# Moving the split of a stream sum behind the last key products' copy, and the gates' bias to the constants, in a one-core encoder block

## The chip, the cores and the metric

The kernel runs on one core of a Trainium2 chip. A core has five engines that run their own instruction queues in order: TensorE (PE, matrix products; PEld is its loading of the fixed operand), VectorE (DVE), ScalarE (ACT), GpSimd (POOL) and SyncE (SP, which here issues most transfers). They wait for each other and for transfers on semaphores. The metric is the device time of one execution in microseconds (us), lower is better. Matrix products accumulate in PSUM, in banks of 128 x 512 float32 values here; a bank is read out ("evicted") by ScalarE or VectorE before another product starts in it.

## The reference, cut to what matters

One block for a sequence of 1024 frames with 16 learned tokens ahead of them (1040 columns), width 1024, all in float32:

```python
h = concatenate([meta, x])                                   # 1040 x 1024
h = h + token_mixer(rmsnorm(h, norm_mix_g))
h = h + channel_mixer(rmsnorm(h, norm_ffn_g))
return rmsnorm(h, norm_final_g)[:, 16:]

# token_mixer: proj = u @ w_in gives, per head,
#   4 mLSTM heads:     q, k (convolution, silu), v, output gate o, and the scalar gates i, f
#   4 retention heads: q, k (rotary), v, output gate g
i_pre = ml_i + ml_b_i
li = 15 * tanh(i_pre / 15)                                   # -1e30 on padding
lf = log_sigmoid(ml_f + ml_b_f)
# a scan over chunks for each head, head_norm, times sigmoid(o) or silu(g), then @ w_out
# channel_mixer: (silu(causal_dwconv(u @ w_up)) * (u @ w_gate)) @ w_down
```

## The kernel before

**Products in three parts.** Each float32 operand is split into a high part (a cast on ScalarE to a shorter float, `AC.copy`) and a low part (the operand less its high part, on VectorE). A product is then three matmuls into one bank: high x high, low x high, high x low (`mm3`, L912, and `mm3s`, L917; the matmuls stand on L913 to L915 and L923 to L925).

**Seven products for eight.** The normalised stream is held transposed as four quarters, "11", "12", "21", "22" (the first digit is the half of the sequence, the second the half of the 1024 channels). Most projections are made with seven products of sums of quarters in place of eight: `ROWS` (L1003) lists which block of the stream each of the products n = 0 to 6 reads: 11, 12, S2, S1, S3, S4, 22. Each product runs in two column chunks (ch0, ch1). It accumulates in a bank of kind x (tag pa or pb) or y (the other). S1 = 22 - 21, and the quarters "21", "11" and "12" are overwritten with further sums (`usum`, L1838; L1843 and L1841 are its two operations on VectorE). `usplit` (L1845) then makes the high part (L1849, ScalarE) and low part (L1850, VectorE) of a sum, in two halves of 128 x 1056 each.

**The stage of the change** (L1786 to L1890, the first 100 us or so). After the norms, the unit runs the products of head 4, the first retention head, without the seven-product scheme: `v4_group` (L945, values and gates, L967) and `q4_group` (L973, i = 0 queries, i = 1 keys). `q4_group` ends with the copy of the bank into `raws[i]`, L979, and leaves that instruction as `last["raw"]`. The last one, for keys and columns 272 to 528 of the second half, is "the last key products' copy". The sums are written in this order: S1 = 22 - 21, then 21, 11 and 12 in place, with the splits of S2 and S1 written ahead of the last `q4_group`s, and those of S3 and S4 after them. S1 lives in the two tiles tagged A1 and A2. A copy of the "12" sum, `x12`, is made into other tiles by ScalarE behind `last["raw"]` (L1869), and S4 is split from it. `tables_load(4)` (L1146, the transfers L1153 and L1154) fills new tiles of the same tags A1 and A2 with the rotary cosines and sines, so the first transfer waits until nobody reads S1 any more.

**The gates.** `gates()` (L1241) turns the i and f columns of all chunks into the scan's weights: two transposes on TensorE (L1258, L1259) into bank pg, a bias scaled by 1/15 (L1262, VectorE), the tanh (L1263, ScalarE, with that bias), the exponential and the logarithm (L1267, L1272), cumulative sums and maxima (L1283, L1285) and transposes (L1290, L1291) with further steps up to L1329. It is a Python generator and is advanced a piece at a time between other work.

**Rotary.** `rotary(i, r)` (L1222) works on head 4's queries (i = 0) and keys (i = 1): two copies on ScalarE that swap the halves of the partitions (L1228, L1229), then two multiplications by the tables A1 and A2 and an addition on VectorE (L1231 to L1233).

**What sets the order.** Instructions written before `pinned[0] = True` (L1888) are put in order by the framework's scheduler, from dependencies and a model of their durations; `after(a, b)` (L105) adds an edge that only keeps a behind b in order and adds no wait if both are on one engine. From L1888 on a hook (`watch`, L132) chains each instruction of TensorE, VectorE and ScalarE to the one written before it on that engine (`before[engine]`), so that order is the written one. `before` is emptied at L1889, so the first of each engine has no predecessor. What is written when is decided by `slot` (L1752) and `go` (L1770): after each step of a product they advance side tasks (gates, rotary, scans) according to the estimated loads of the engines in `load` and the limits in `RULES`. SyncE's and GpSimd's transfers and the instructions written before the pin stay with the framework's scheduler and may be put among pinned ones.

**Weights.** `quartered` (L555) gives the seven weight blocks of a head; `parts` (L472) casts them (L474, `hi_...`) and makes their low parts (L479, `lo_...`), and L567 to L572 make the sums of weights in place. The raw weights of head 4's output gate are raw_o4a and raw_o4b, those of the next head's queries and keys raw_q0a and raw_q0b; a raw tile is loaded again (L328) once its last reader is done. `evac` (L1017) evicts a product's bank: by ScalarE for n = 0, 6 (L1019) and n = 2, 3 (L1021), by VectorE for the others (L1023).

**Start.** L271 loads the vector constants into `vec` from ScalarE's queue, L273 sets one more column of it, and the first VectorE work after that is the square of L859.

## Time and profile before

| | |
|---|---|
| median of 3 runs | 1531.71 us (1531.26 to 1532.25) |
| profiled execution, its own time | 1529.36 us |
| span from the first to the last instruction | 1527.6 us |
| mean granted clock of TensorE | 0.995 |
| busy: TensorE, VectorE, ScalarE | 97%, 71%, 50% of the span |
| TensorE in 72 to 75 us | 1.04 of 3.00 us busy |
| TensorE in 90 to 94.4 us | 0.00 of 4.40 us busy |
| TensorE in 99 to 103 us | 3.20 of 4.00 us busy |

How to read the rows. In a row of the order of time stand the start (us from the span's start), the duration (us), the engine, the line of the kernel, the operation, the tile written <- the tiles read, the shapes, the count, and in brackets how long the engine was idle before and what it then waited for. A name with q, such as SPq, is the engine's queue issuing a transfer. A row with a count over 1 covers several instructions in sequence. In the table of waits stand who waited, for whom, the total in us, how many times, and the longest. In a row by stretches of time stand the length, then busy us and instruction counts of PE, PEld, DVE, ACT and POOL, the granted clock, the share of the transfer engines, and GB/s. The time of a matmul's row is longer than its share of TensorE, since matmuls overlap: the distance between two starts counts. Tile names: rawq and rawk are head 4's queries and keys, sig its output gate, uS1h and uS1l the high and low parts of S1, po4x and po4y the banks of head 4's output products, s the tiles of S1 or of the copied sum, A the rotary tables, gts, gates and gsm the gates' tiles, qT and kT the rotated queries and keys.

### The profile page before, as it was taken

How to read it: one execution, taken by the hardware profiler on the slowest of the kernel's cores; microseconds unless marked ns; L12 is line 12 of the kernel's file. 1: busy time of each engine (PE TensorE's matmuls, PEld its weight loads, DVE VectorE, ACT ScalarE, POOL GpSimd, SP SyncE). 2: the span in 40 equal slices, each digit the busy share in tenths (PEclk: the TensorE clock that was granted, in tenths of full speed). 3: DMA queues.
4: the chain of work that ended last, by engine and by line, in shares of the span. 5: the costliest groups of instructions: out<-in, count | busy, mean ns of one | idle time of the engine just before them, and what ended most of it. 6: DMA issues, size and time to landing. Idle time of an engine off the chain costs nothing.

```text
span 1527.6 us, 25490 instructions
## 1 busy us (share of the span) xinstructions
PE 1488.0 (97%) x9929; PEld 1349.2 (88%) x9929; DVE 1089.4 (71%) x2087; ACT 756.4 (50%) x1455; POOL 72.2 (5%) x157
## 2 busy tenths in 40 slices
PE   7989999999999999999999999999999999999997
PEld 7978999999999999987888988999999999888887
DVE  6875868678777677746868688767666666778657
ACT  4465655554655445553454465444444444434443
POOL 1000000000000000000000001222220000000000
PEclk9999999999999999999999999999999999999999
DMA  6022256323532455697333237778872224933313
GB/s 232 2 85 58 82 166 194 108 80 118 174 131 91 132 166 178 203 385 271 110 110 135 80 119 229 205 201 206 193 185 77 83 77 155 375 102 113 97 42 111
DMA packets 104586, 223.81 MB, mean 147 GB/s; under 512 B 10520, under 2 KB 33760, under 8 KB 104288
## 3 DMA queue, kind: packets, MB, share of 16 engines
q1 hardware_dynamic: 89824, 191.68, 37.7%
q0 software_dynamic: 8448, 23.07, 7.5%
q10 hardware_dynamic: 6192, 7.41, 1.4%
q8 instruction: 78, 1.28, 0.4%
q14 instruction: 44, 0.36, 0.1%
HBM read 178.05 MB, written 67.15 MB: 161 GB/s over the span
## 4 chain that ended last, share of the span: by engine, by line
PE 88%; DVE 6%; DMA 3%; ACT 2%; issue 1%; SPq 0%; ACTq 0%; DVEq 0%
PE pdx L925 3%; PE pdx L924 3%; PE pdx L923 3%; PE pup_x L924 2%; PE pup_x L925 2%; PE pga_x L923 2%; PE pup_x L923 2%; PE pga_x L924 2%; PE pga_x L925 2%; PE pdy L925 2%; PE pdy L924 2%; PE pdy L923 2%; PE n L1621 2%; PE pwx L925 2%; PE u L1619 2%; PE pwx L923 2%
## 5 line engine op out<-in xcount | busy, mean ns | idle before, releaser
L782 ACT CAST hi_up<-raw_up 128x512 fp32r<-128x512 f32 (+1 forms) x52 | 36.5, 719 | 107.7 <-PE pga_z L924 61.1
L783 DVE TENSOR_TENSOR lo_up<-raw_up,hi_up 128x512 fp32r<-128x512 f32 (+1 forms) x52 | 41.2, 809 | 38.3 <-ACT hi_up L782 37.6
L923 PE MATMUL pup_x<-uh_g,hi_up 128*128 128x256 f32 (+1 forms) x240 | 67.2, 282 | 1.2 <-ACT uh_g L1989 1.2
L783 DVE TENSOR_TENSOR lo_ga<-fraw_ga,hi_ga 128x512 fp32r<-128x512 f32 (+1 forms) x52 | 41.8, 807 | 37.1 <-ACT hi_ga L782 36.9
L924 PE MATMUL pup_x<-ul_g,hi_up 128*128 128x256 f32 (+1 forms) x240 | 67.4, 282 | 0.1
L925 PE MATMUL pup_x<-uh_g,lo_up 128*128 128x256 f32 (+1 forms) x240 | 66.4, 282 | 0.0
L783 DVE TENSOR_TENSOR lo_d<-rd,hi_d 128x1024 fp32r<-128x1024 f32 (+1 forms) x34 | 37.6, 1112 | 32.8 <-ACT hi_d L782 32.7
L782 ACT CAST hi_ga<-fraw_ga 128x512 fp32r<-128x512 f32 (+1 forms) x52 | 36.4, 719 | 45.3 <-PE pup_z L924 23.9
L925 PE MATMUL pdx<-uh_d,lo_d 128*128 128x512 f32 (+1 forms) x156 | 57.9, 375 | 0.0
L924 PE MATMUL pdx<-ul_d,hi_d 128*128 128x512 f32 (+1 forms) x156 | 57.8, 374 | 0.0
L782 ACT CAST hi_d<-rd 128x1024 fp32r<-128x1024 f32 (+1 forms) x34 | 32.3, 959 | 49.2 <-PE pdy L924 32.5
L925 PE MATMUL pdy<-uh_d,lo_d 128*128 128x512 f32 x132 | 51.9, 393 | 0.0
L924 PE MATMUL pdy<-ul_d,hi_d 128*128 128x512 f32 x132 | 51.7, 392 | 0.0
L923 PE MATMUL pdx<-uh_d,hi_d 128*128 128x512 f32 (+1 forms) x156 | 48.5, 372 | 0.0
L923 PE MATMUL pdy<-uh_d,hi_d 128*128 128x512 f32 x132 | 47.9, 389 | 0.0
L923 PE MATMUL pga_x<-uh_g,hi_ga 128*128 128x512 f32 x120 | 47.5, 396 | 0.0
L924 PE MATMUL pga_x<-ul_g,hi_ga 128*128 128x512 f32 x120 | 47.5, 396 | 0.0
L923 PEld LDWEIGHTS pup_x<-uh_g,hi_up 128*128 128x128 f32 x240 | 45.3, 189 | 2.3 <-ACT uh_g L1989 1.4
L925 PE MATMUL pga_x<-uh_g,lo_ga 128*128 128x512 f32 x120 | 47.1, 393 | 0.0
L924 PEld LDWEIGHTS pup_x<-ul_g,hi_up 128*128 128x128 f32 x240 | 45.4, 189 | 1.0 <-DVE ul_g L1990 0.3
L925 PEld LDWEIGHTS pup_x<-uh_g,lo_up 128*128 128x128 f32 x240 | 44.7, 189 | 0.8
L1688 DVE SCALAR_TENSOR_TENSOR mx<-tr,vec,sig 128x386 f32<-128x386 f32 (+2 forms) x42 | 24.0, 571 | 21.2 <-PE tr L1680 16.1
(1687 smaller groups left out, 5730.6 us busy)
## 6 DMA issues: line engine op xcount, KB each, us to landing
raw_up<-w_up_d SPq DMA_DIRECT2D x22, 512.0 KB, 4.2
fraw_ga<-w_gate_d SPq DMA_DIRECT2D x22, 512.0 KB, 4.3
acts<-cv SPq DMA_DIRECT2D x44, 256.0 KB, 4.4
wsd<-w_down_d POOLq DMA_DIRECT2D x44, 256.0 KB, 6.6
rd<-wsd SPq DMA_DIRECT2D x22, 512.0 KB, 3.6
raw_w<-w_out_d SPq DMA_DIRECT2D x20, 512.0 KB, 7.5
wsw<-raw_w SPq DMA_DIRECT2D x32, 256.0 KB, 3.7
raw_m<-w_out_d SPq DMA_DIRECT2D x14, 512.0 KB, 4.1
```

The lines of the kernel that those rows point to most:

```text
L782: AC.copy(hi[:, o:o + n], x)
L783: V.tensor_tensor(lo[:, o:o + n], x, hi[:, o:o + n].bitcast(F32), ALU.subtract)
L923: m.append(PE.matmul(pt, ah, xh_, start=first and k == 0, stop=False, skip_group_check=True))
L924: PE.matmul(pt, ah, xl_, start=False, stop=False, skip_group_check=True)
L925: m.append(PE.matmul(pt, al, xh_, start=False, stop=last and k == n - 1, skip_group_check=True))
L1619: PE.matmul(up[:, :nv], kw[:L], v, start=True, stop=True)
L1621: PE.matmul(pn[:L, :nv], pt[:L, :L], v, start=True, stop=c == 0)
L1688: return V.scalar_tensor_tensor(dst, tr[:, x0 - t0:x1 - t0], vec[:, g:g + 1], sig(b, p)[:, x0 - a0:x1 - a0], ALU.mult, ALU.mult)
```

## The change

Three edits, in the diff in full:

1. The split of S1 is written after the last `q4_group` and not before it. Each cast of S1 is kept behind the last key products' copy on ScalarE; each cast and low part of S3 is kept behind the last of S1's on its engine; the copies of the "12" sum are kept behind S3's casts in place of the key copy.
2. The first ScalarE instruction written after the pin is kept behind S1's last cast.
3. The scaled bias of the gates is computed at the start of the kernel into a column of `vec` that was unused, by the same VectorE operation, and `gates()` reads it from there.

```diff
--- before.py
+++ after.py
@@ -271,6 +271,7 @@
     AC.dma_start(vec[:, :V_N], vecs)
     xload(0)
     V.memset(epsc, EPS)
+    V.tensor_scalar(vec[:R36, V_N + 1:V_N + 2], vec[:R36, V_BI:V_BI + 1], 1.0 / 15.0, None, ALU.mult)
     warm = tmp.tile([P, 5], F32, tag="rcol", name="warm")
     AC.activation(warm[:, 0:1], epsc, AF.Sqrt)
     nc.sync.dma_start(cs, cst)
@@ -1258,8 +1259,7 @@
         PE.transpose(pg[:R36, 0:P], gts[:, 0].rearrange("p a b -> p (a b)"), ident)
         PE.transpose(pg[:R36, P:2 * P], gts[:, 1].rearrange("p a b -> p (a b)"), ident)
         li, x, ax, w, lf = row("li"), row("x"), row("ax"), row("w"), row("lf")
-        bi = small(R36, 1)
-        V.tensor_scalar(bi, vec[:R36, V_BI:V_BI + 1], 1.0 / 15.0, None, ALU.mult)
+        bi = vec[:R36, V_N + 1:V_N + 2]
         AC.activation(li, pg[:R36, 0:P], AF.Tanh, bias=bi, scale=1.0 / 15.0)
         V.tensor_scalar(x, pg[:R36, P:2 * P], vec[:R36, V_BF:V_BF + 1], None, ALU.add)
         V.tensor_scalar(ax, x, -1.0, None, ALU.mult)
@@ -1846,15 +1846,19 @@
         ublock_pair(nm, th, tl)
         for i in range(2):
             h_, l_ = (u[:, 2 * i:2 * i + 2] for u in UB[nm])
-            AC.copy(h_, part(x, i))
-            V.tensor_tensor(l_, part(x, i), h_.bitcast(F32), ALU.subtract)
+            m = last["hi", nm] = AC.copy(h_, part(x, i))
+            n = last["lo", nm] = V.tensor_tensor(l_, part(x, i), h_.bitcast(F32), ALU.subtract)
+            if nm == "S1":
+                after(m, last["raw"])
+            elif nm == "S3":
+                after(m, last["hi", "S1"])
+                after(n, last["lo", "S1"])
 
     usum(0, "22", "21", "S1")
     usum(0, "11", "21", "21")
     usum(1, "S1", "11", "11")
     usplit("S2", "11", "r0", "r1")
     usum(1, "11", "12", "12")
-    usplit("S1", "S1", "uh3", "ul3")
     need(("o", 4, 1), 0)
     for i in range(2):
         q4_group(i, 1, 16, 272, next(ring0))
@@ -1862,11 +1866,12 @@
         v4_group(c, next(ring0))
     for i in range(2):
         q4_group(i, 1, 272, SB, next(ring0))
+    usplit("S1", "S1", "uh3", "ul3")
     usplit("S3", "21", "r2", "r3")
     x12 = [vslot(2 + i, f"s4_{i}").rearrange("p (k j) -> p k j", k=2) for i in range(2)]
     tables_load(4)
     for i in range(2):
-        after(AC.copy(x12[i], part("12", i)), last["raw"])
+        after(AC.copy(x12[i], part("12", i)), last["hi", "S3"])
     s1[:] = x12
     need(("o", 4, 1))
     usplit("S4", "S1", "uh2", "ul2")
@@ -1887,6 +1892,7 @@
     done["tr"] = 0.0
     pinned[0] = True
     before.clear()
+    before["Activation"] = last["hi", "S1"].ins.name
     go(o_steps(4))
     for p, (a, b) in enumerate(PAIRS):
         side += sig_tasks(prev) if p else sig_tasks(4)
```

## The prediction

> **What bounds the kernel now.** I read the page's first part, then the table of waits of TensorE, then the time-ordered rows of each engine around the places that table names.

> ```profile
> PE 1488.0 (97%) x9929; PEld 1349.2 (88%) x9929; DVE 1089.4 (71%) x2087; ACT 756.4 (50%) x1455; POOL 72.2 (5%) x157
> ...
> PE po4y L923 <- ACT sig L1021: 4.6, 1, 4.6
> ...
> PE po4x L923 <- ACT rawk L979: 2.0, 1, 2.0
> ```

> TensorE (PE) is busy for 97% of the span, so only its idle time, 1527.6 - 1488.0 = 39.6 us, can be won. The diff touches one stage, about 57 to 103 us, and these two waits lie in it, 4.6 and 2.0 us, with two short ones whose rows come below. The longer is TensorE's wait before n = 5 of head 4's output products, and its rows show what lies behind it:

> ```profile
> 94.41 0.39 PE L923 MATMUL po4y<-uS4h,hi_o 128*128 128x258 f32 x1 [4.57 <-ACT sig L1021]
> 94.00 0.63 ACT L1021 ACTIVATE sig<-po4y 128x256 f32<-128x256 f32 x2
> 92.44 0.36 ACT L1263 ACTIVATE gates<-pg,gsm 36x128 f32<-36x128 f32 x1
> 91.15 1.28 ACT L1263 ACT_TABLE_LOAD   x1 [2.88 <-DVE gsm L1262]
> 90.94 0.13 DVE L1262 TENSOR_SCALAR gsm<-vec 36x1 f32<-36x1 f32 x1
> 88.20 0.71 DVE L1232 TENSOR_TENSOR kT<-kT,A 128x528 f32<-128x528 f32 x1 [2.21 <-DMA A<-rot_d]
> 81.12 0.39 SPq L1154 DMA_DIRECT2D A<-rot_d  x1
> ```

> Read it downward, backwards in time. The bank's eviction stands behind the tanh in ScalarE's (ACT) queue; the tanh waits for a bias that VectorE (DVE) scales at 90.94; VectorE had stood for the second rotary table, issued at 81.12. That table reuses the tile of the stream's first sum, S1, whose casts and low parts come late:

> ```profile
> 71.18 2.05 ACT L1849 CAST uS3h<-x 128x1056 fp32r<-128x1056 f32 x2 [0.57 <-PE pq L915]
> 73.13 1.13 ACT L474 CAST hi_o<-raw_o4b 128x512 fp32r<-128x512 f32 x2
> 74.17 0.36 ACT L979 COPY rawk<-pq 128x256 f32<-128x256 f32 x1
> 74.43 2.05 ACT L1869 COPY s<-x 128x1056 f32<-128x1056 f32 x2
> 76.39 0.36 ACT L1019 COPY sig<-po4x 128x258 f32<-128x258 f32 x1
> 76.65 2.05 ACT L1849 CAST uS1h<-s 128x1056 fp32r<-128x1056 f32 x2
> 78.86 2.06 ACT L1849 CAST uS4h<-s 128x1056 fp32r<-128x1056 f32 x2
> 78.14 2.42 DVE L1850 TENSOR_TENSOR uS1l<-s,uS1h 128x1056 fp32r<-128x1056 f32 x2
> 72.22 0.28 PE L915 MATMUL pq<-u22h,lo_q 128*128 128x256 f32 x1
> ```

> The last key product ends at 72.22 + 0.28 = 72.50, but S3's casts and two weight casts hold its copy until 74.17; that is the 2.0 us wait.

> **The change part by part.** *The key copy.* S3's casts now follow S1's, which follow the copy. The copy can start at 72.50, or, if the two weight casts (73.13 to 74.17, 1.04 us) still go ahead of it, at 73.54. TensorE resumes 0.4 us after a copy starts (74.17 to 74.58), at 72.9 to 73.95, so 0.6 to 1.7 us of the 2.0 go. That lead is lost again at n = 3:

> ```profile
> 83.89 0.39 PE L925 MATMUL po4y<-uS1h,lo_o 128*128 128x258 f32 x1 [0.51 <-DVE lo_o L479]
> 83.15 1.28 DVE L479 TENSOR_TENSOR lo_o<-raw_o4a,hi_o 128x512 fp32r<-128x512 f32 x2
> 89.56 0.28 PE L925 MATMUL po4x<-uS3h,lo_o 128*128 128x256 f32 x1
> ```

> Those low parts stand behind S4's on VectorE, so I need the new place of S4.

> *ScalarE's queue.* From 71.18 on it worked without a pause until here:

> ```profile
> 83.57 0.34 ACT L936 COPY vz<-pvm 16x256 f32<-16x256 f32 x1
> 86.07 0.63 ACT L1228 COPY rawq<-rawk 64x528 f32<-64x528 f32 x1 [2.16 <-DVE qT L1231]
> 87.65 0.61 ACT L474 CAST hi_o<-raw_q0a 128x512 fp32r<-128x512 f32 x1
> 85.28 0.71 DVE L1231 TENSOR_TENSOR qT<-rawq,A 128x528 f32<-128x528 f32 x1 [0.84 <-DMA A<-rot_d]
> 92.84 0.34 DVE L1264 TENSOR_SCALAR gates<-pg,vec 36x128 f32<-36x128 f32 x1 [1.77 <-ACT gates L1263]
> ```

> That is 83.91 - 71.18 = 12.73 us of work. In the new order nothing large may start before 72.50, so it ends at 85.23: 1.3 us later, a real cost of the new order. Then come the rotary copies, one eviction and one weight cast (86.07 to 87.65 + 0.61 = 88.26, 2.19 us), to 87.42; with no bias to wait for, the table load follows, and from its start to VectorE's first gate step are 92.84 - 91.15 = 1.69 us. Bound by ScalarE: 89.11.

> *VectorE.* S1's first cast (half of 2.05) follows the key copy (74.17 to 74.43, 0.26) and is done at 73.8; its two low parts take 2.42, so S1 is dead at 76.2 (77.3 with the weight casts ahead) instead of 78.14 + 2.42 = 80.6, and both tables can be issued by then. The second took 88.20 - 81.12 = 7.1 us to land, so both are there by 83.3 (84.4). Then come S3's low parts, 2.42 (to 78.6), and up to 2.5 of two weight low parts, one weight sum (about 0.64 each, half of the 1.28 above) and two evictions (to 81.1). S4's casts start after rawk, S1, S3 and the copies of the second sum (0.26 + 3 x 1.96 = 6.14), at 78.6, or 80.2 with the casts and evictions that stood among them; its low parts start one cast later, 79.8 to 81.3, and end at 82.2 to 83.7, the two weight low parts (1.28) at 83.5 to 85.0. So the first rotary product starts at 83.5 to 85.0 instead of 85.28. ScalarE's copies start 0.79 later and VectorE's gate step 0.79 + 2.19 + 1.69 = 4.67 after it: 88.2 to 89.7.

> The later of the two bounds decides: 89.1 to 89.7 against 92.84, **3.1 to 3.7 us earlier; I take 3.4**.

> *What TensorE makes of it.* n = 5 starts 94.41 - 92.84 = 1.57 after that step, at 90.7 to 91.3; TensorE reaches it after the n = 3 low part (half of 1.28 past S4's, 82.8 to 84.3) plus 89.7 - 83.9 = 5.8, at 88.6 to 90.1. The 4.6 us shrink to 0.6 to 2.7. Its clock gains too:

> ```profile
> 94.40:99.00 4.60, 4.59 (x25) 4.59 (x26) 4.46 (x11) 3.57 (x6) 0.00 (x0) 0.63 0.00 0
> ...
> 98.89 0.28 PE L923 MATMUL po4x<-u22h,hi_o 128*128 128x258 f32 x1
> 86.82 0.28 PE L923 MATMUL po4x<-uS3h,hi_o 128*128 128x258 f32 x1
> 126.67 0.49 PE L1574 MATMUL s<-qT,kT 128*128 128x128 f32 x2 [2.47 <-DVE pt L1598]
> ```

> After the 4.57 us of idle the granted clock is 0.63, and n = 5 takes 98.89 - 94.41 = 4.48 us where n = 4 took 2.86 (23 intervals in 89.56 - 86.82 = 2.74, so 24 of 0.119): 1.62 us lost. After 1.96 (74.58) and 2.47 us (126.67) no matmul is slow. With the short wait that loss should go. I do not add it, because of who is late next:

> ```profile
> 101.46 0.42 DVE L1283 TENSOR_TENSOR_SCAN gates<-gates 36x128 f32<-36x128 f32 x1
> 102.88 0.19 PE L1291 MATMUL pe<-cs,gsm 36*1 36x36 f32 x1 [0.76 <-DVE gsm L1287]
> 114.17 0.68 DVE L479 TENSOR_TENSOR lo_q<-raw_q0b,hi_q 128x512 fp32r<-128x512 f32 x1
> 114.88 2.00 SPq L328 DMA_DIRECT2D raw_vp<-w_vp_d  x2
> 124.83 1.14 ACT L474 CAST hi_vp<-raw_vp 128x512 fp32r<-128x512 f32 x2 [4.97 <-DMA raw_vp<-w_vp_d]
> ```

> From 92.84 to 102.68 VectorE works the gates through without a pause, and TensorE's transposes for them wait for it. So what passes 103 us is VectorE's shift, 3.4. The same chain frees the slot for the load at 114.88 that holds ScalarE until 124.83 and TensorE until 126.67: that 2.5 us wait moves along whole. Behind it all is TensorE's work, and 3.4 us stay won.

> [...]

> *The bias step at the start.* It is one VectorE instruction of 0.13 us that now waits for the vector load.

> ```profile
> vec<-vecs_d ACTq DMA_DIRECT2D x1, 70.0 KB, 2.9
> 4.98 0.76 DVE L859 TENSOR_TENSOR sqr<-x 128x576 f32<-128x576 f32 x1 [4.11 <-DMA x<-h_in_d]
> ```

> The load, issued at 0.74, lands by 3.6; the square queued behind it stands until 4.98 for x. Cost nothing; without that cover it is 0.13. The added order costs no wait between engines. The first output eviction (76.39) must now follow S1's casts (74.8): it is needed at n = 2, past 78 us. S3 is needed at n = 4 (86.82 before, 85.9 at the earliest now) and S4 at 90.7; both are done by 83.7.

> Against the profiled execution's own 1529.36 us the sum gives 1526.0. The median of the runs shown is 1531.71; 3.4 below it is **1528.3**.

> **The rivals.** *The loads do not come forward.* S1 may free its tile early and the tables still stand in SyncE's queue behind weight loads. Then only the bias goes: VectorE's gate step starts where the bias stood, 90.94; gain 1.9, 1529.8. Against it: S1 dead 3.3 to 4.4 us earlier.

> *A weight load takes the tables' place.* The cast of raw_q0a stands ahead of the tanh on ScalarE.

> ```profile
> 76.84 0.33 SPq L328 DMA_DIRECT2D raw_q0a<-w_g_d  x1
> 84.46 0.80 SPq L328 DMA_DIRECT2D raw_q0b<-w_g_d  x2
> ```

> Its load waits for the weight low part that VectorE makes after S3's, which the diff pushes back; S4's lows and the evictions could push it further. Issued at 80 to 82 it lands (5 to 7 us) by 85 to 89 against the 86.8 at which the cast wants it: gain 1.2 to 3.4, around 2.4, 1529.3. Behind raw_q0b, past 85.3, it lands at 90 to 92.4. **The other side:** past 90.3 the whole gain is used up and each further us is a us lost; issued at 88, with 7 us, landing at 95, it is 4.7 slower, 1536.4; at 85.3, 2.1 slower.

> *The low clock comes back where nothing hides it.* TensorE now waits 1.5 to 2.1 us for the scan (101.88 - 3.4 = 98.5, n = 6 ending two times 2.86 after 90.7 to 91.3, at 96.4 to 97.0), does one short transpose and waits 0.76 again: 2.3 to 2.9 us, between the 2.47 that cost nothing and the 4.57 that cost 1.62. If it does cost that, the gain is 1.8, 1529.9.

> *More than forecast.* The wait at 126.67 also shrinks, because the loads ahead of it spread: up to 2.5 more, gain 5.9, 1525.8.

> **How the numbers follow.** Forecast 0.55; tables not forward 0.12; late weight load but still a gain 0.12; low clock 0.08; more 0.05; slower than before 0.08, half of it by little. The likeliest case gives 1528.3. Leaving out the tails of "more" and of "slower", the range is 1526.6 to 1531.4. A measurement of this kernel tells about 0.2%, 3.1 us, from no change: the forecast's 3.1 to 3.7 is just past it, and the runs' own spread of 1.0 us can put it on either side, so 0.47 of the 0.55 count as faster, with 0.05 of "more": 0.52. The middle cases and half of "slower" make same 0.43; slower 0.05.

> **What would show it.** Right: the key copy before S3's casts; S1's casts done by 76, both table loads issued by 77.5; no wait of the tanh on VectorE; its gate step near 89.3; the 4.6 us wait at most 2.7 and n = 5 at full clock; 2 to 3 us of waiting at the gates' transposes; the score row of 126.67 near 123.3. Wrong: raw_q0a landing after 87; or a different order of the queues later on, which would move waits past 130 us that I take as unchanged.

## The result and the profile after

The changed kernel is **faster** by 0.3%, a difference clear of the spread between executions but far below 2%: 1525.82 us in the median of 6 runs (1524.53 to 1527.52), against 1531.39 us of the kernel before beside it (6 runs, 1529.03 to 1532.25); ratio 0.9968, 95% interval 0.9955 to 0.998. Repeated in the longest comparison, it had 1525.78 us (9 runs, 1523.14 to 1527.96) against 1530.06 us (27 runs, 1526.0 to 1532.85); ratio 0.9977 (0.9967 to 0.9987). The medians are 5.6 us apart in the first comparison and 4.3 in this one. The profiled execution took 1525.64 us.

The head of its page: the span, then busy time and share of each engine.

```profile
span 1523.9 us, 25488 instructions
...
PE 1487.8 (98%) x9929; PEld 1349.9 (89%) x9929; DVE 1090.4 (72%) x2087; ACT 756.4 (50%) x1455; POOL 72.1 (5%) x157
```

TensorE's work is the same; its idle time went from 39.6 to 1523.9 - 1487.8 = 36.1 us. The table of its waits in the changed kernel says where (total, times, longest):

```profile
PE po4y L924 <- ACT sig L1022: 1.7, 1, 1.7
PE pe L1290 <- DVE gates L1283: 1.6, 1, 1.6
...
PE po4x L924 <- ACT rawk L980: 1.3, 1, 1.3
...
PE tr L1680 <- DVE mx L1688: 1.2, 1, 1.2
...
PE po4x L924 <- ACT sig L1020: 0.6, 1, 0.6
```

The wait before n = 5 went from 4.6 to 1.7, that for the key copy from 2.0 to 1.3, and the 0.5 before the n = 3 low part is gone. New are 1.6 at the first transpose of the gates and 0.6 before n = 2, whose bank now waits for an eviction behind S1's and S3's casts and x12's copies. The fourth row lies 300 us further on, in the head norms; in the table of before it reads:

```profile
PE tr L1680 <- DVE mx L1688: 2.5, 4, 1.1
```

More of that below.

The stage in order of time, to be read against the same rows of before (lines here are one higher from L274 to L1259):

```profile
73.54 0.36 ACT L980 COPY rawk<-pq 128x256 f32<-128x256 f32 x1
73.80 2.05 ACT L1849 CAST uS1h<-s 128x1056 fp32r<-128x1056 f32 x2
77.52 0.33 SPq L1155 DMA_DIRECT2D A<-rot_d  x1
83.04 0.71 DVE L1233 TENSOR_TENSOR kT<-kT,A 128x528 f32<-128x528 f32 x1 [0.28 <-DMA A<-rot_d]
87.48 1.28 ACT L1263 ACT_TABLE_LOAD   x1
89.17 0.34 DVE L1264 TENSOR_SCALAR gates<-pg,vec 36x128 f32<-36x128 f32 x1 [0.98 <-ACT gates L1263]
90.75 0.39 PE L924 MATMUL po4y<-uS4h,hi_o 128*128 128x258 f32 x1 [1.66 <-ACT sig L1022]
98.27 0.19 PE L1290 MATMUL pe<-cs,gates 36*1 36x36 f32 x1 [1.55 <-DVE gates L1283]
99.22 0.21 PE L1291 MATMUL pe<-cs,gsm 36*1 36x36 f32 x1 [0.77 <-DVE gsm L1287]
102.93 0.19 DVE L1305 TENSOR_TENSOR gsm<-gsm 1x36 f32<-1x36 f32 x1
103.19 1.28 ACT L1306 ACT_TABLE_LOAD   x1 [6.07 <-DVE gsm L1305]
104.49 0.23 ACT L1306 ACTIVATE gsm<-gsm 1x36 f32<-1x36 f32 x1
112.55 2.01 SPq L329 DMA_DIRECT2D raw_vp<-w_vp_d  x2
124.18 0.49 PE L1574 MATMUL s<-qT,kT 128*128 128x128 f32 x2 [2.23 <-DVE pt L1598]
```

Down to 90.75 this is the forecast in its own order: the two weight casts still went ahead of the key copy (73.54), S1's casts follow, the second table is issued at 77.52 in place of 81.12, the tanh waits for nothing, and the gate step stands at 89.17 in place of 92.84, **3.67 earlier**. VectorE carries the lead on whole: L1305, its last step ahead of the exponential, comes 106.59 - 102.93 = 3.66 earlier. Then something is lost on ScalarE. At the exponential of L1306 the lead is only 106.81 - 104.49 = 2.32, at the weight load whose slot this chain frees 114.88 - 112.55 = 2.33, and at the score row 126.67 - 124.18 = 2.49. The same place in the kernel before, in order of time, and then a row that the view of that line by itself has in the changed kernel and not in this one (its 17 ns, and its start):

```profile
102.32 1.28 ACT L1306 ACT_TABLE_LOAD   x1
106.59 0.18 DVE L1305 TENSOR_TENSOR gsm<-gsm 1x36 f32<-1x36 f32 x1
106.81 0.23 ACT L1306 ACTIVATE gsm<-gsm 1x36 f32<-1x36 f32 x1 [3.21 <-DVE gsm L1305]
```

```profile
L1306 ACTq EVENT_SEMAPHORE  x1: 17/17/17, 103.1 to 103.1; - x1
```

Before, the table load ran at 102.32, under the wait, and only the ACTIVATE stood for VectorE. Now an extra semaphore instruction stands ahead of the load, the load itself waits for VectorE (6.07 us), and its 1.28 us lie on the chain.

For the whole kernel I counted TensorE's matmuls in order and took the time between the k-th ones in the profiled executions (us; the 820th is the score row, 2850 to 3000 holds the head norms at about 395 to 407):

| matmuls | before | before, again | after | after, again |
|---|---|---|---|---|
| 0 to 820 | 119.5 | 120.0 | 117.1 | 117.1 |
| 820 to 1700 | 116.5 | 118.0 | 116.5 | 116.1 |
| 2850 to 3000 | 19.8 | 19.2 | 18.4 | 18.4 |
| 5250 to 5320 | 22.7 | 21.6 | 21.6 | 21.5 |
| 6400 to 6600 | 32.8 | 34.3 | 34.3 | 32.8 |
| all | 1513.4 | 1514.7 | 1509.8 | 1507.7 |

So 2.4 to 2.9 us come from the stage and 0.8 to 1.4 from the head norms, both in every pair. The other rows differ by 1 to 1.5 us between executions of one and the same kernel.

### The profile page after: what moved, and what is told of

Same layout as the page of the kernel before. It is cut to its first block, busy times and chain, and to the rows that moved or that the text cites. A ratio compares the mean times of both kernels' runs of the same rounds, so it can differ in the third digit from the quotient of the medians.

```text
span 1523.9 us, 25488 instructions
## 1 busy us (share of the span) xinstructions
PE 1487.8 (98%) x9929; PEld 1349.9 (89%) x9929; DVE 1090.4 (72%) x2087; ACT 756.4 (50%) x1455; POOL 72.1 (5%) x157
## 3 DMA queue, kind: packets, MB, share of 16 engines
q8 instruction: 78, 1.28, 0.3%
## 4 chain that ended last, share of the span: by engine, by line
PE 89%; DVE 5%; ACT 2%; DMA 2%; issue 1%; SPq 0%; DVEq 0%; ACTq 0%
PE pdx L926 3%; PE pdx L925 3%; PE pdx L924 3%; PE pup_x L925 2%; PE pup_x L924 2%; PE pup_x L926 2%; PE pga_x L924 2%; PE pga_x L925 2%; PE pga_x L926 2%; PE pdy L926 2%; PE pdy L925 2%; PE pdy L924 2%; PE n L1621 2%; PE pwx L926 2%; PE u L1619 2%; PE pwx L924 2%
## 5 line engine op out<-in xcount | busy, mean ns | idle before, releaser
L925 PE MATMUL pup_x<-ul_g,hi_up 128*128 128x256 f32 (+1 forms) x240 | 67.7, 284 | 0.1
L784 DVE TENSOR_TENSOR lo_d<-rd,hi_d 128x1024 fp32r<-128x1024 f32 (+1 forms) x34 | 37.7, 1113 | 32.8 <-ACT hi_d L783 32.7
L925 PE MATMUL pdx<-ul_d,hi_d 128*128 128x512 f32 (+1 forms) x156 | 57.8, 374 | 0.0
L925 PE MATMUL pdy<-ul_d,hi_d 128*128 128x512 f32 x132 | 51.7, 392 | 0.0
L925 PE MATMUL pga_x<-ul_g,hi_ga 128*128 128x512 f32 x120 | 47.5, 396 | 0.0
L925 PEld LDWEIGHTS pup_x<-ul_g,hi_up 128*128 128x128 f32 x240 | 45.8, 191 | 1.0 <-DVE ul_g L1996 0.3
```

Source lines behind the costliest of these rows:

```text
L784: V.tensor_tensor(lo[:, o:o + n], x, hi[:, o:o + n].bitcast(F32), ALU.subtract)
L925: PE.matmul(pt, ah, xl_, start=False, stop=False, skip_group_check=True)
```

## The experiments

**Theory.** The moved split carries the stage's gain, the exponential's table load takes 1.3 of it back, and the rest of the time's difference is a gain at the head norms that depends on when the kernel arrives there, together with a base that the three runs put too high. **Rivals:** the bias alone does it; the low clock at the gates' transposes is what is lost; the pinned order's new edge (edit 2) does something of its own. The kernel before ran beside them in three series: 1530.06 us in the median beside the first four (27 runs, 1526.0 to 1532.85), 1530.30 beside the next four (25 runs, 1527.85 to 1532.8), 1530.17 beside the last two (16 runs, 1526.33 to 1533.21). Each ratio is against its own series.

**Edits 1 and 2 without the bias** (split_only):

```diff
-    V.tensor_scalar(vec[:R36, V_N + 1:V_N + 2], vec[:R36, V_BI:V_BI + 1], 1.0 / 15.0, None, ALU.mult)
...
-        bi = vec[:R36, V_N + 1:V_N + 2]
+        bi = small(R36, 1)
+        V.tensor_scalar(bi, vec[:R36, V_BI:V_BI + 1], 1.0 / 15.0, None, ALU.mult)
```

> The gates' bias is put back into the gates (scaled by VectorE just ahead of the tanh); the moved split and its order stay. Theory (the gates' chain carries the gain, the bias is only worth what VectorE is late): the bias is scaled after VectorE's three additions, at about 88.2, the table load of the tanh starts at 88.4 and VectorE's gate step at 90.1, 2.7 us ahead of before and 0.9 behind the changed kernel. The exponential's table load at L1306 still waits for VectorE, so 1.3 of that is lost and the score row of before's 126.67 is 1.4 us early. Time 0.9 to 1.3 us above the changed kernel. Rival (the split alone does nothing, the bias is what counts): gate step at 92 to 93, time as before.

Measured 1526.67 us (11 runs, 1524.42 to 1528.12), ratio 0.9976 (0.9968 to 0.9985). Its stage in order of time:

```profile
89.84 0.34 DVE L1264 TENSOR_SCALAR gates<-pg,vec 36x128 f32<-36x128 f32 x1 [1.79 <-ACT gates L1263]
103.86 1.28 ACT L1306 ACT_TABLE_LOAD   x1 [4.56 <-DVE gsm L1305]
124.47 0.49 PE L1574 MATMUL s<-qT,kT 128*128 128x128 f32 x2 [2.42 <-DVE pt L1598]
```

The gate step is 3.00 earlier than before, of the 3.67 of the whole change, and the table load waits here too. The split carries the gain; the bias adds 0.67 at the gate step and 0.29 at the score row.

**The bias alone** (bias_only): before with edit 3 only.

```diff
+    V.tensor_scalar(vec[:R36, V_N + 1:V_N + 2], vec[:R36, V_BI:V_BI + 1], 1.0 / 15.0, None, ALU.mult)
...
-        bi = small(R36, 1)
-        V.tensor_scalar(bi, vec[:R36, V_BI:V_BI + 1], 1.0 / 15.0, None, ALU.mult)
+        bi = vec[:R36, V_N + 1:V_N + 2]
```

> Only the bias is moved to the constants, the split stays where it was. Theory: VectorE's gate step starts where its bias step stood, at 90.9, 1.9 us ahead of before; the exponential's table load at L1306 is free to run ahead as it did before, so the whole 1.9 reaches the score row (124.8). The wait before n = 5 shrinks from 4.6 to 2.7. Time 1.9 us below before. Rival (the tables hold everything and the bias is hidden behind them): no change.

Measured 1527.42 us (11 runs, 1525.95 to 1530.68), ratio 0.9984 (0.9976 to 0.9993). The stage missed what was expected of it; rows in order of time, then a stretch of time (length, busy us of PE, PEld, DVE, ACT, POOL, and the granted clock, third from the end):

```profile
74.93 0.39 PE L924 MATMUL po4x<-u11h,hi_o 128*128 128x256 f32 x1 [1.96 <-ACT rawk L980]
79.66 0.42 DVE L1024 TENSOR_TENSOR sig<-sig,po4y 128x258 f32<-128x258 f32 x1 [2.50 <-PE po4y L926]
93.29 0.34 DVE L1264 TENSOR_SCALAR gates<-pg,vec 36x128 f32<-36x128 f32 x1
127.06 0.49 PE L1574 MATMUL s<-qT,kT 128*128 128x128 f32 x2 [0.94 <-DVE pt L1598]
```

```profile
76.10:79.50 3.40, 3.40 (x18) 3.40 (x17) 1.06 (x2) 3.40 (x6) 0.00 (x0) 0.51 0.39 101
```

In this execution the 1.96 us wait for the key copy, the same as before, was followed by 3.4 us at half clock. VectorE then stood 2.50 us for the slow product, and all behind it on its queue came later; the gate step and score row came 0.4 later than before. This execution's own time is the median of the eleven, 2.6 us below the kernel before, so what it gains doesn't lie in the stage: against the first profile of before, the stretch from matmul 2850 to 3000 is 1.0 us shorter (18.8) and that from 5250 to 5320 1.1 (21.6), which before itself reaches in its second profile. What the bias alone is worth in a stage without the slow stretch stays open.

**The exponential's tile** (dr_in_dec): the changed kernel, with the exponential's operand in a row of a tile that is there anyway, not in a new small one.

```diff
-        dr = small(1, R36)
+        dr = dec[:1]
```

> The changed kernel with one row of the gates (the decays dr, 1 x 36) kept in the tile dec in place of gsm, so that the exponential of L1306 has one semaphore to wait for and its table load none. Theory (the table load that now waits for VectorE costs 1.3 us on the gates' chain): the table load runs before 100, the exponential starts at 103.1 in place of 104.5, and the score row comes at 122.8 to 123.0 in place of 124.2; time 1.2 us below the changed kernel. Rival (the low clock of 99 to 102.5 is what was lost, 1.4 us, and TensorE is the bound there): the exponential earlier, the score row still at 124.2.

Measured 1524.76 us (7 runs, 1522.4 to 1526.72), ratio 0.997 (0.996 to 0.9981). Its rows in order of time:

```profile
97.30 1.28 ACT L1306 ACT_TABLE_LOAD   x1
103.32 0.24 ACT L1306 ACTIVATE dec<-dec 1x36 f32<-1x36 f32 x1 [4.73 <-DVE dec L1305]
123.48 0.49 PE L1574 MATMUL s<-qT,kT 128*128 128x128 f32 x2 [1.28 <-DVE pt L1598]
```

The load runs ahead at 97.30 and waits for nothing, the ACTIVATE starts 1.17 earlier than in the changed kernel, the score row 0.70 (0.5 later than the latest that was expected). Against the kernel before, the lead is 3.49 at the exponential and 3.19 at the score row. The extra semaphore instruction of L1306 is gone; split_only and key_first have it as the changed kernel does, bias_only and before don't. So the operand's tile, together with the moved casts, decides whether the table load carries the wait. Why the new tile does isn't shown by a run. The median is 1.0 us below the repeat of the changed kernel's, and the intervals overlap.

**The changed kernel again** (after_again), no edit.

> The changed kernel once more, unchanged. Theory (the profiled span's 3.7 us is the change's size, and the 5.6 us between the medians is spread of the runs, since both kernels' runs lie within about 3 us): the gate step again at 89.2 and the exponential at 104.5 to within 0.1, but waits or low-clock stretches past 390 us that come and go by 1 to 1.5 us; in these rounds 3.5 to 5 us below before. Rival (5.6 is the size and the profile of before was a lucky one): 5 to 6 us in these rounds too, and before's runs at 1531 to 1532.

Measured 1525.78 us. In order of time the marks of its stage lie within 0.2 us of the first profile's; its profiled execution, 1523.49 us, is 2.15 shorter: the row 6400 to 6600 has 1.5 of it, a low clock at 919 to 922 (0.72 over 918 to 924) that this execution doesn't have (1.00 over 916 to 922).

```profile
89.00 0.34 DVE L1264 TENSOR_SCALAR gates<-pg,vec 36x128 f32<-36x128 f32 x1 [0.99 <-ACT gates L1263]
124.02 0.49 PE L1574 MATMUL s<-qT,kT 128*128 128x128 f32 x2 [2.23 <-DVE pt L1598]
```

**The kernel before again** (before_again), no edit.

> The kernel before, once more, unchanged. Theory (what the two profiles differ by past 390 us is spread between executions): the same waits up to 130 us to within 0.2 us (4.6 before n = 5, gate step 92.8, score row 126.7), and at least one of the three later places different: the score transposes' waits at 395 to 407 us (1.2 in all), the low clock at 712 to 720 (0.50), none at 921. Time 1526 to 1532.9, median about 1530. Rival (they belong to the kernel before): all three as in the first profile.

Measured 1531.33 us (10 runs, 1528.47 to 1532.77), ratio 1.0008 (0.9998 to 1.0017): one program differs from itself by 1.0 us in the medians of 10 and 25 runs. All three later places came out different, as the theory had it. The stage didn't repeat to 0.2 us: TensorE waited 5.0 before n = 5, not 4.6, and the score row came 0.29 later. That row, and two stretches of time with a low clock:

```profile
126.96 0.49 PE L1574 MATMUL s<-qT,kT 128*128 128x128 f32 x2 [2.15 <-DVE pt L1598]
```

```profile
95.00:102.00 7.00, 6.96 (x38) 6.96 (x38) 6.67 (x20) 4.21 (x7) 0.00 (x0) 0.60 0.00 0
...
126.00:131.00 5.00, 4.04 (x16) 3.63 (x17) 3.91 (x11) 1.53 (x5) 0.00 (x0) 0.69 0.00 0
```

In the first profile of before, the second of these places runs at 1.00:

```profile
126.00:131.00 5.00, 4.33 (x28) 4.09 (x29) 4.30 (x13) 1.60 (x5) 0.00 (x0) 1.00 0.00 0
```

This is the 1.5 us by which the table's row 820 to 1700 differs within one kernel; row 6400 to 6600 differs by as much, with a clock of 0.72 over 921 to 927 here and 1.00 over 920 to 926 in the first profile.

**No low clock at the transposes** (keep_warm): the changed kernel with 12 matmuls ahead of the first transpose of the gates, written into an unused part of its bank, which nobody reads, and left out of the planner's loads.

```diff
...
+        for _ in range(12):
+            PE.matmul(pe[:, 256:512], UB["11"][0][:, 0, 0:P], UB["11"][0][:, 0, 0:256], start=True, stop=True)
...
```

> The changed kernel with twelve matmuls of 128x256 whose results nobody reads ahead of the gates' transposes, in the 1.6 us in which TensorE waited for the scan. Theory (the low clock of 99 to 102.5 costs 1.4 us of TensorE's time, but the chain through the gates' exponential and the load of 112.6 is what ends at the score row): the clock stays at 1.0 there, the head's products run 1.4 us earlier, the wait before the score row grows from 2.2 to 3.6 us, the score row stays at 124.2 and the time is that of the changed kernel. Rival (TensorE's lateness is what was lost): the score row at 122.8, time 1.4 us below the changed kernel.

Measured 1527.93 us (10 runs, 1525.73 to 1528.26), ratio 0.9983 (0.9973 to 0.9992). In the changed kernel, the transposes' waits are followed by a stretch of half clock, as its stretches of time show; the second fence has this kernel's, the third its rows in order of time.

```profile
98.60:99.10 0.50, 0.00 (x0) 0.00 (x0) 0.47 (x3) 0.00 (x0) 0.00 (x0) 0.98 0.00 0
...
99.10:102.50 3.40, 3.28 (x15) 3.21 (x16) 3.34 (x12) 0.00 (x0) 0.00 (x0) 0.50 0.00 0
...
102.50:103.00 0.50, 0.50 (x6) 0.50 (x5) 0.43 (x5) 0.00 (x0) 0.00 (x0) 1.00 0.00 0
```

```profile
99.00:103.00 4.00, 3.40 (x28) 3.36 (x29) 3.91 (x14) 0.00 (x0) 0.00 (x0) 1.00 0.00 0
...
123.00:127.00 4.00, 2.92 (x10) 2.47 (x10) 3.29 (x9) 1.27 (x4) 0.00 (x0) 0.68 0.02 4
```

```profile
105.16 0.41 PE L1316 MATMUL pf<-gsm,cs 1*128 1x36 f32 x2 [0.81 <-ACT gsm L1313]
124.08 0.49 PE L1581 MATMUL s<-qT,kT 128*128 128x128 f32 x2 [2.32 <-DVE pt L1605]
```

The stretch at 99 to 103 is at full clock, and the score row has moved by 0.10: TensorE waits elsewhere for the same chain, here 0.81 for the exponential's results. So the low clock there costs nothing up to the score row, and this rival falls. The wait before the score row stayed at 2.32, where 3.6 had been expected, and the median is 2.2 us above that of the repeat of the changed kernel, where the same time had been: this execution has another low stretch behind the score row, and its head norms take 19.2 us, not 18.4.

**Only the key copy first** (key_first): before, with S3's casts kept behind the last key products' copy; S1's split stays where it was.

```diff
-            AC.copy(h_, part(x, i))
+            m = AC.copy(h_, part(x, i))
...
+            if nm == "S3":
+                after(m, last["raw"])
```

> The kernel before with one edge: S3's casts behind the last key products' copy; S1's split and the bias as before. Theory (the 2.0 us wait for the key copy is hidden behind the later wait before n = 5): the copy starts at 72.5 or 73.5 and the wait for it falls to 0.3 to 1.3 us, but S1 and the tables come no earlier, so the wait before n = 5 grows by as much and the score row stays at 126 to 128; time within 1 us of before. Rival (the key copy is what the change wins by): 1 to 2 us faster.

Measured 1528.48 us (10 runs, 1526.57 to 1530.63), ratio 0.9987 (0.9978 to 0.9997). In order of time:

```profile
78.09 2.05 ACT L1849 CAST uS1h<-s 128x1056 fp32r<-128x1056 f32 x2
94.65 0.39 PE L923 MATMUL po4y<-uS4h,hi_o 128*128 128x258 f32 x1 [2.57 <-ACT sig L1021]
127.92 0.49 PE L1574 MATMUL s<-qT,kT 128*128 128x128 f32 x2 [2.65 <-DVE pt L1598]
```

The wait for the key copy falls from 2.0 to 1.3, but S1's casts come 1.44 later than before and n = 5 0.24 later: up to there the key copy gains nothing by itself. The score row is 1.25 later, and most of that is the exponential's table load, which stands behind VectorE here as in the changed kernel (at 107.08, idle 4.52 before it) and puts the exponential 1.57 later. The time is still 1.8 us lower at the median, against less than 1 expected; this profile, 1529.23 us, doesn't place it, and its interval almost reaches 1.

**Without edit 2** (no_pin_edge):

```diff
-    before["Activation"] = last["hi", "S1"].ins.name
```

> The changed kernel without its second edit, so that the first output eviction may run ahead of S1's casts. Theory: the eviction (0.26 us) goes ahead of S1's casts, everything behind it on ScalarE is at most 0.3 us later, S4's casts move past one eviction and one copy; gate step 89.0 to 89.8, time that of the changed kernel to within 0.5 us. Rival (the edge is what keeps S1 early): S1's casts 1 us or more later and the tables with them, half of the gain lost.

Measured 1524.40 us (4 runs, 1523.62 to 1525.43), ratio 0.9963 (0.9948 to 0.9978). In order of time the first output eviction now goes ahead of S1's casts:

```profile
74.20 0.38 ACT L1020 COPY sig<-po4x 128x258 f32<-128x258 f32 x1
74.46 2.06 ACT L1849 CAST uS1h<-s 128x1056 fp32r<-128x1056 f32 x2
124.18 0.49 PE L1574 MATMUL s<-qT,kT 128*128 128x128 f32 x2 [1.76 <-DVE pt L1598]
```

S1's casts are 0.66 later, the wait of 0.6 before n = 2 is gone, and the score row is where it was. The median of these four runs is 1.4 us below the changed kernel's, more than the 0.5 expected. Edit 2 gains nothing that this measurement sees.

**Arriving later at the head norms** (late_2us): the changed kernel with 20 matmuls ahead of a score row of head 4's scan (chunk 6), into an unused part of its bank, which nobody reads, and left out of the planner's loads.

```diff
...
+        if (h, c) == (4, 6):
...
+            for _ in range(20):
+                PE.matmul(s[:, 256:512], UB["11"][0][:, 0, 0:P], UB["11"][0][:, 0, 0:256], start=True, stop=True)
...
```

> The changed kernel with twenty matmuls of 128x256 that nobody reads ahead of the seventh score row of head 4, some 2.4 us of TensorE's work after the stage of the change. It delays everything behind it by about what the change had won up to the score row. Theory (arriving earlier is worth more than the 2.5 us, because at 395 to 407 us the transposes' waits on VectorE hang on the absolute time of arrival): the stretch from matmul 2850 to 3000, 18.4 us in the four profiles of the changed order and 18.7 to 19.8 in the kernels that arrive 2 us later, becomes 18.7 to 19.8 here; time 2.4 to 3.5 us above the changed kernel, within 1 us of before. Rival (those waits come and go by chance, or belong to the order of the queues): 18.4 here too, and the time 2.4 us above the changed kernel.

Measured 1526.38 us (10 runs, 1525.5 to 1527.87), ratio 0.9978 (0.9969 to 0.9987). The added row in order of time, and the head norms' waits in the table of waits:

```profile
133.15 2.56 PE L1580 MATMUL s<-u11h 128*128 128x256 f32 x20
```

```profile
PE tr L1688 <- DVE mx L1696: 1.8, 2, 1.3
```

The stretch from 2850 to 3000 takes 19.1 us, as the theory had it, against 18.4 in both profiles of the changed kernel, with the same order of instructions. So part of that gain hangs on when TensorE arrives. The other profiles agree: of all twelve, the five that reach this stretch by 387.6 us take 18.4 to 18.5, the seven that reach it from 389.2 us on take 18.7 to 19.8, and three of these seven (split_only, keep_warm, late_2us) have the changed order of the casts. The total missed: 0.6 us above the repeat of the changed kernel, where 2.4 to 3.5 had been expected. Its profiled execution is 1526.17 us, 0.5 above the first of the changed kernel and 2.7 above the second, so the medians, 10 and 9 runs with spreads of 2.4 and 4.8 us, don't settle this.

**Both mends together** (both_mends): dr_in_dec and no_pin_edge in one kernel.

> The changed kernel with the decays' row kept in the tile dec and without the second edit. Theory (the exposed table load costs 0.7 us at the score row and the second edit nothing or less): the table load of L1306 ahead of VectorE's steps, exponential at 103.3, score row at 123.3 to 123.6 against 124.2; time 0.5 to 1.5 us below the changed kernel, so 1524 to 1525.3. Rival (the 1524.4 and 1524.8 of the two kernels one by one are runs with few low-clock stretches): 1525 to 1526, as the changed kernel.

Measured 1524.74 us (6 runs, 1524.6 to 1526.09), ratio 0.9969 (0.9958 to 0.998). In order of time:

```profile
102.94 0.23 ACT L1306 ACTIVATE dec<-dec 1x36 f32<-1x36 f32 x1 [3.19 <-DVE dec L1305]
122.35 0.72 PE L1574 MATMUL s<-qT,kT 128*128 128x128 f32 x2 [2.02 <-DVE pt L1598]
```

The stage gains 1.8 us more at the score row, 0.95 us earlier than the earliest that was expected, and the median is 1.0 to 1.1 below the changed kernel's, no more than either mend alone. All three lie far below the kernel before; among themselves, and against the changed kernel, the intervals don't part them.

## Why the prediction was wrong, and where it was right

The sign was right and the size near: 3.4 us is 0.0022 of the time, and both ratios' intervals hold it, the first close to its edge. That is luck in part: the stage gave 2.5 in place of 3.4, and the head norms, which the sum has at nothing, gave 1.1. The time, 1525.82 us, lies 0.8 below the low end of the range. Two terms of the sum failed: the base, and the waits past 130 us, which it takes as unchanged. A third, the shift that stays won, was too large.

- **The key copy, the tables, the gate step: right.** The copy came at the later of its two places (73.54). The gate step, forecast at 89.1 to 89.7, came at 89.17; it was ScalarE's bound that decided, with the tanh's table load at 87.48 where 87.42 was forecast. VectorE's own path came in another order than forecast: S4's casts started at 82.67, behind the rotary copies, not at 78.6 to 80.2, and S4's low parts ended at 86.8, not by 83.7. The first two rotary multiplications went ahead of them, from 82.06, so VectorE still had 0.98 us to spare at the gate step. n = 5, forecast at 90.7 to 91.3 with a wait of 0.6 to 2.7, came at 90.75 with 1.66; the transposes' waits, 2.3 to 2.9 in all, were 1.55 + 0.77. The late weight load did not happen: raw_q0a was issued at 75.12. The bias step at the start ran at 3.60, while VectorE still had 1.14 us to wait for x. The first output eviction, taken as early enough, made TensorE wait 0.6 before n = 2; no_pin_edge shows that this doesn't reach the score row.
- **"3.4 us stay won": too large.** VectorE's shift did pass 103 us, with 3.66 at L1305. But 2.49 came out at the score row, because the exponential's table load, which the prediction doesn't mention and which lay under a wait before, now stands on the chain (1.28 us). dr_in_dec shows it: with the load ahead of the wait again, 3.19 come out.
- **The low clock.** The rival with a chance of 0.08 came to pass as an event: 3.4 us at 0.50 after 1.55 and 0.77 us of waiting. Its cost did not: keep_warm takes it away and the score row stays. That the prediction kept the clock's gain out of the sum was right for the reason it gave, the gates' chain.
- **"Waits past 130 us that I take as unchanged": wrong by 0.8 to 1.4 us**, at the head norms. late_2us and the twelve profiles show that the time of arrival counts there; which transfer or engine turns it stays open.
- **The term that put the time below the range is the base.** "The median of the runs shown is 1531.71; 3.4 below it is 1528.3": three series of the same kernel have medians of 1530.06, 1530.30 and 1530.17, and all its 84 runs together, before_again's with 1531.33 among them, have 1530.4. So the base was 1.3 to 1.7 high, and forecast and range with it; 1.5 lower, the range holds the measured time. From 1530.2, with the stage's 2.5 and the head norms' 1.1, comes 1526.6. The 0.8 us that remain are not placed; one program differs from itself by 1.0 in before_again. The short comparison by itself can't tell base from gain: there the kernel before has 1531.39 in six runs, three of them the prediction's own, and the same miss looks like a gain of 5.6. The profiled execution's 1529.36 stood in the prediction, gave 1526.0, and was the better base. And the range, built from cases inside the stage, left out that executions of one program spread by some 5 to 7 us; its low end was too near.

## What to carry to other kernels

Work the gain out on the profiled execution's own time, and let the range hold the spread of single executions beside that of the cases; three runs that agree to 1 us can still lie 1.3 to 1.7 us off a longer series. When instructions are moved, look at the activations behind them that load a table: here the moved casts put the exponential's load behind the wait that had covered it (103.19 in place of 102.32, 1.28 us more on the chain), and another tile for the operand put it ahead again (97.30). An idle engine freed early at one place is worth what the next chain lets through: here 3.67 us at the gate step, 2.5 at the next common point.

## What the runs showed of the hardware

**The length of one wait didn't tell here whether a low clock follows it.** TensorE's wait before the score row was followed by a stretch of half clock at 2.15 us in before_again (mean clock 0.69 over 126 to 131) and at 2.42 us in split_only (0.76 over 124 to 131), and by none at 2.23 us in the changed kernel (1.00 over 124 to 129), 2.47 us in before (1.00 over 126 to 131) and 2.65 us in key_first (1.00 over 126 to 132). The 1.96 us wait for the key copy came out both ways too: 0.51 over 76.10 to 79.50 in bias_only, 1.00 over 71.05 to 91.53 in before.

The waits that came out both ways fit this. Before the score row of before, the wait from 124.20 to 126.67 was divided between two steps with 1.95 and 2.41 us busy. In before_again the half clock began at about 127.9 (an estimate: 0.69 over 126 to 131 is 3.1 us at half), so the wait from 124.81 to 126.96 lay whole in the 3.41 us ahead of it, with at most 1.26 us busy. In bias_only it began at about 76.04 (an estimate: 0.94 over 75.60 to 76.10), so the 1.96 us up to 74.93 lay whole in one step, with at most 1.45 us busy; in before the wait for the key copy reached past the end of its step, which had 1.57.

So the length of a wait of 1.5 to 2.5 us didn't decide by itself here: one and the same kernel came out on both sides, before with 2.47 us and full clock, before_again with 2.15 us and half. A stretch of 3.41 us at half clock is worth up to 1.7 us, an estimate: half of 3.41. The one behind the 4.57 us wait made n = 5 take 4.48 us where n = 4 took 2.86, 1.62 more.
